# Weights split by the DMA that loads them: high parts rounded on the way in, low parts added onto the negated high parts

## The chip, the cores and the metric

The kernel runs on one core of a Trainium2 chip. The metric is the device time of one execution in microseconds (us), the median over the runs shown. A profile of one execution of the kernel before is at hand; times inside the kernel come from it.

## What is computed

One layer of a transformer block over 528 tokens (16 meta tokens and 512 real ones) of width 1024: an RMS norm, a projection into three attention branches (stick-breaking, indexed sparse with a top-k of 132 keys, differential) and three gates, the branches' output projections, an output matrix, a second norm and a gated feed-forward network with a convolution of width three. Cut to the two functions that hold the dense products:

```python
def _mixer(u, layer, w_in, ...):
    (q_sb, k_sb, v_sb, q_sp, k_sp, v_sp, q_ix, k_ix, w_ix,
     q_df, k_df, v_df, g_sb, g_sp, g_df) = _split_cols(u @ w_in)
    ...
    merged = (sigmoid(g_sb + b) * (y_sb @ w_br_sb) + sigmoid(g_sp + b) * (y_sp @ w_br_sp)
              + sigmoid(g_df + b) * (y_df @ w_br_df))
    return merged @ w_out

def _conv_ffn(u, w_up, conv_w, conv_b, w_down):
    z = u @ w_up
    gate, val = z[..., :D_FF], z[..., D_FF:]
    gp = jnp.pad(gate, ((0, 0), (CONV_WIDTH - 1, 0), (0, 0)))
    conv = conv_b + sum(gp[:, i:i + tp] * conv_w[i] for i in range(CONV_WIDTH))
    return (jax.nn.silu(conv) * val) @ w_down
```

All inputs are float32.

## The kernel before, in words

Activations lie transposed, features on the partitions, tokens along the free dimension. The weights are packed into 133 chunks of [128, 1024] float32, 512 KB each: eight tiles of 128 by 128. TensorE multiplies in the format float32r. To keep the precision of float32, every operand is split into a high part (the value rounded to float32r) and a low part (the value minus its high part), and every product is made in three passes: high by high, weight-high by activation-low, weight-low by activation-high (`mm3`, L309). A chunk of eight k-tiles is so 24 matmuls per half of the tokens; the low parts of its weights are read by the third pass alone.

The chunks are streamed in a fixed order (`order`, L277 to L287). `load` (L291) fetches a chunk with a DMA from SyncE's queue into a tile `wr` (three buffers). `prep` (L297) makes the two parts: ScalarE casts `wr` into `wh` (L304), and `sub` (L105) forms `wl = wr - wh` on VectorE or GpSimd, whichever a rough clock kept by the program takes to be free sooner; `wh` and `wl` have two buffers each. Every dense product first calls `prep` for its own chunk and for the next one, so that the split runs a chunk ahead, and `prep` starts the load two chunks ahead.

The first two chunks (`W_IX`, `W_QIX`) go along with the arrival of the input: the eight input tiles `hT` and halves of the two chunks alternate on SyncE's queue (L345 to L356), and a loop over the eight k-tiles (L382) emits, for each, the norm gain and split of the input tile (`xh` on ScalarE, `xl` on VectorE), at tiles 0, 1 and 4 the split of a part of the two chunks (`split`, L360: a cast on ScalarE, a subtraction on VectorE), the square of the tile for the norm, and 12 matmuls (`step`, L365).

TensorE runs in the order in which instructions are emitted: dense products with matmuls of attention streams between them, placed by the rough clock. The other engines run in order too; a tile framework sets the order on each of them from the emission order, its own estimate of when an instruction can start, and priorities, and puts in the semaphore waits. Two lines stand for many instructions in the profile, because helpers issue them: L97 for every operation of VectorE, ScalarE and GpSimd (`Timed.run`), L179 for every matmul (`mm`); L119 is `gdma`, a DMA issued by GpSimd. Groups are told apart by their tiles.

The feed-forward part (L1122 to L1142) runs 22 pairs of chunks. The gate chunk's product is evacuated by VectorE into `ft` tiles, convolved (one ScalarE operation, two on VectorE) and passed through SiLU on ScalarE; the value chunk's product is evacuated by VectorE, multiplied by the gate on GpSimd (`ft<-ft`, L1140), cast into `ah` on ScalarE and reduced to `al` by `sub`. The last 22 chunks multiply `ah` and `al` down to the output.

```python
    def prep(k):
        ...
        S.copy(wh, r)
        sub(wl, r, wh, HVW)
        wsp[k] = (wh, wl)
        load(after.get(after.get(k)))
```

Of the kernel before, what the change touches and what calls it, by code (L numbers as in the profile page):

```python
# [15 lines left out]
P = 128  # L16
D = 1024
T = 528            # meta tokens and real tokens
NM = 16
Q0 = 14            # first token whose mixer output is needed (the convolution reaches back two)  # L20
TQ = T - Q0        # 514 queries
HQ = TQ - 256      # 258: two meta queries and query blocks 0 and 1
# [11 lines left out]
# columns of the packed small parameters  # L34
# [4 lines left out]
# chunks of [128, 1024] in the packed weights  # L39
# [4 lines left out]
# the mixer's dense products in order: the projections of two heads' worth of a branch, four tiles  # L44
# of gates, half the columns of a branch's output
# [10 lines left out]
def tile_kernel(ctx: ExitStack, tc, hT, wpk, par, bias, yT):  # L56
# [3 lines left out]
    # ------------------------------------------------------------- order of emission  # L60
    # TensorE runs in the order in which its instructions are emitted here: dense products, with
    # the matmuls of other streams of work between them. A rough clock of the engines tells when a
    # stream's operands will be there, so that its matmuls come no earlier.
# [4 lines left out]
    SLACK = 1800    # from an operand's making by the clock to its matmul  # L68
    BSL = 500       # from a bank's last reading by the clock to its next use
    PACE = 12000    # for a round of the top-k  # L70
    TKS = 10000     # from the index part's making to its first product
    PRI = 100       # by how many instructions an evacuation goes ahead
    SET = 2200      # by how much earlier than SLACK the other engines' dependent steps come
    HVW = 1000      # VectorE's handicap against GpSimd for the weights' low parts
    HV = 500        # and for other differences
# [28 lines left out]

    def sub(out, a, b, hv=HV):  # L105
        """a - b in SBUF on VectorE, or on GpSimd where that is free sooner"""
        t = clock["P"]
        tv = max(clock["V"], t) + V.cost(out) + hv
        e = G if max(clock["G"], t) + G.cost(out) < tv else V
        e.tensor_tensor(out, a, b, OP.subtract)  # L110
# [16 lines left out]
    # ------------------------------------------------------------------ pools  # L127
# [13 lines left out]
    def bank(tag):  # L141
        """a PSUM bank, when one is free by the clock"""
        while sum(h["t"] + BSL > clock["P"] for h in held[tag]) >= banks[tag]:
            yield
        h = {"t": math.inf}
        held[tag].append(h)
        return ps.tile([P, 512], F32, tag=tag, bufs=banks[tag], name="ps" + tag), h
# [4 lines left out]
    # Slots that several streams of work share. A slot is taken here before the instructions  # L152
    # that fill it are emitted and given back after the last that reads it is, so an engine that
    # runs in the order of emission can't wait for one that is given back later.
# [30 lines left out]
    # ------------------------------- streams, which run between a dense product's matmuls  # L185
# [14 lines left out]
    def side_by_side(gens):  # L200
        """several streams in one; what each returns"""
# [16 lines left out]
    def settle(more=0):  # L218
        """until what the stream has emitted is done"""
# [4 lines left out]
    def ease(most=3000):  # L224
        """while VectorE is far behind"""
        while clock["V"] > clock["P"] + most:
            yield
# [11 lines left out]
    # -------------------------------------------------------------- constants  # L239
# [19 lines left out]
    # causal mask of a query block of 128 against columns c, the key at c standing at c - 400  # L259
    # from the block's first query  # L260
# [8 lines left out]
    # the two meta queries (14 and 15) against the meta keys  # L269
# [4 lines left out]
    # ------------------------------------------------------- weights, streamed  # L274
# [15 lines left out]

    def load(k):  # L291
        if k is not None and k not in wraw:
            r = wp.tile([P, 8, P], F32, tag="raw", bufs=3, name=f"wr{k}")
            nc.sync.dma_start(r, wpk[k].rearrange("p (j c) -> p j c", c=P))
            wraw[k] = r

    def prep(k):  # L297
# [3 lines left out]
        r = wraw[k]  # L301
        wh = wp.tile([P, 8, P], F32R, tag="wh", bufs=2, name=f"wh{k}")
        wl = wp.tile([P, 8, P], F32R, tag="wl", bufs=2, name=f"wl{k}")
        S.copy(wh, r)  # L304
        sub(wl, r, wh, HVW)
        wsp[k] = (wh, wl)
        load(after.get(after.get(k)))

    def mm3(out, prs, xh, xl, start=True, stop=True):  # L309
        """out += w^T x for the tiles j of chunk k and k-tiles kt of x, in three exact passes"""  # L310
# [13 lines left out]
    HALF = ((0, TH), (TH, TH))           # all tokens  # L324
    HALQ = ((0, HQ), (HQ, 256))          # queries, counted from token Q0

    # ------------------------------------------------ the input, and its norm's factors
# [3 lines left out]
    take("tmp", 10)  # L331
    for k in (W_IX, W_QIX):
        wraw[k] = wp.tile([P, 8, P], F32, tag="raw", bufs=3, name=f"wr{k}")
        wsp[k] = tuple(wp.tile([P, 8, P], F32R, tag=t, bufs=2, name=f"{t}{k}") for t in ("wh", "wl"))
# [6 lines left out]
    def load_half(k, a):  # L341
        nc.sync.dma_start(wraw[k][:, a:a + 4], wpk[k].rearrange("p (j c) -> p j c", c=P)[:, a:a + 4])

    # the order that gives TensorE work from the first tile of the input on
# [16 lines left out]
    def split(k, a, b):  # L361
        r, (wh, wl) = wraw[k], wsp[k]
# [3 lines left out]
    def step(k, ds, halves, q0, kt):  # L366
        """one k-tile of a tile of all its columns"""
# [12 lines left out]
    # the first two tiles go along with the input's arrival  # L380
# [17 lines left out]
    def rstd(dst, st, y0, a, now=True):  # L398
        """dst = (v + eps)^-0.5 from st = -v/2 in PSUM: Exp and Ln, then a Newton step"""
# [15 lines left out]
    # ------------------------------------------------ factors from the small parameters  # L415
# [6 lines left out]
    # -lambda of the differential attention on every partition  # L422
# [10 lines left out]
    # ------------------------------------- relative bias, by how far a key lies from the query  # L433
# [5 lines left out]
    def bias_stream():  # L439
# [3 lines left out]
        for e, r in enumerate(brd):  # L443
            # the table's high and low parts above each other, and the buckets of half the distances
# [14 lines left out]
        # a copy for each query, for the steps along which bias_tile reads  # L459
# [5 lines left out]
    def bias_tile(h):  # L465
        """[p, c]: the bias of query p against the key at column c (that is key c - 400 from the
        block's first query), or -1e30 where the key lies ahead"""
# [5 lines left out]
    # ----------------------------------------------------- dense tile of tokens  # L473
# [14 lines left out]
    # ---------------------------------------------------------------- index part  # L488
# [34 lines left out]
    for g in range(2):  # L523
# [15 lines left out]
        # the high, low and again the high parts of each head above each other, by way of DRAM  # L539
# [7 lines left out]
    # Each query's TOPK keys of the best score. Of the first block's 144 keys, the 144 - TOPK of the  # L547
# [684 lines left out]
```

## Time and profile before

| | |
|---|---|
| median of 3 runs | 931.87 us |
| lowest and highest run | 929.49 and 934.09 us |
| profiled execution: span from its first to its last instruction | 928.0 us |
| profiled execution: own time outside the span | not recorded; the median of the runs is 3.87 us above the span |
| TensorE matmuls busy | 901.2 us, 97% of the span, 6054 instructions |
| VectorE, ScalarE, GpSimd busy | 559.4, 456.7, 314.5 us (60%, 49%, 34%) |
| DMA engines | 91.44 MB, a mean of 99 GB/s |

A busy time of TensorE says that it was never without a matmul in flight, not that it ran at its peak. Idle time of an engine counts only where something that sets the end waits for it.

### The profile page before, as it was taken

What the parts mean: (1) busy time and instruction counts of PE and PEld (TensorE: products, weight loads), DVE (VectorE), ACT (ScalarE), POOL (GpSimd) and SP (SyncE); (2) the same over time, 40 slices, a digit from 0 to 9 for tenths busy, and PEclk for the clock granted to TensorE, in tenths of its full rate; (3) what the DMA queues carried; (4) which work ended last, traced back from release to release, by engine and by line L of the source; (5) the groups of instructions that cost most, each with busy time, mean ns of one, the idle gap of its engine ahead of it and who ended that gap; (6) DMA issues with size and microseconds to landing.
All of it is one profiled execution on the core that took longest, in us unless ns stands there. A gap on an engine that the chain in (4) does not pass through costs nothing.

```text
span 928.0 us, 15349 instructions
## 1 busy us (share of the span) xinstructions
PE 901.2 (97%) x6054; PEld 814.3 (88%) x6054; DVE 559.4 (60%) x1129; ACT 456.7 (49%) x848; POOL 314.5 (34%) x185
## 2 busy tenths in 40 slices
PE   7989989899999999999998999999999999999998
PEld 6987988799998889988998999999999999888886
DVE  6599999985578655797437445555555555422221
ACT  7476686668377787644545444333333333311110
POOL 2433232343433424666235323344444333200100
PEclk9999999999999999999999999999999999999999
DMA  6584112142333212331222532223223233333330
GB/s 227 149 237 156 47 69 69 48 125 66 101 104 92 82 63 80 99 97 48 68 78 87 178 91 91 92 91 91 91 91 91 92 96 95 106 113 102 114 102 23
DMA packets 30439, 91.44 MB, mean 99 GB/s; under 512 B 3929, under 2 KB 4073, under 8 KB 30368
## 3 DMA queue, kind: packets, MB, share of 16 engines
q1 hardware_dynamic: 29648, 88.05, 31.0%
q0 software_dynamic: 720, 2.42, 0.9%
q8 instruction: 47, 0.77, 0.3%
q14 instruction: 24, 0.20, 0.1%
HBM read 80.88 MB, written 5.86 MB: 93 GB/s over the span
## 4 chain that ended last, share of the span: by engine, by line
PE 77%; DVE 14%; DMA 4%; ACT 2%; issue 1%; SPq 1%; POOL 0%; DVEq 0%; POOLq 0%; ACTq 0%
PE psd L179 52%; PE psw L179 23%; DVE tmp L97 7%; DVE work L97 2%; DVE m L97 2%; PE psw L183 2%; ACT tmp L97 1%; DMA qd<-tmp 1%; DVE G L97 1%; DMA qk<-qk 1%; DVE pm L97 1%; DMA wr<-wpk 1%; DVE pt L97 1%; DMA qst<-qd 1%; DMA gd<-tab 1%
## 5 line engine op out<-in xcount | busy, mean ns | idle before, releaser
L97 POOL TENSOR_TENSOR wl<-wr,wh 128x1024 fp32r<-128x1024 f32 x75 | 181.3, 2418 | 347.7 <-ACT wh L97 226.7
L97 ACT CAST wh<-wr 128x1024 fp32r<-128x1024 f32 (+2 forms) x137 | 139.2, 1018 | 178.4 <-PE psd L179 123.6
L179 PE MATMUL psd<-xh,wh 128*128 128x258 f32 (+2 forms) x792 | 119.5, 291 | 3.7 <-DVE tmp L97 2.5
L179 PE MATMUL psd<-xh,wl 128*128 128x258 f32 (+2 forms) x792 | 118.6, 290 | 0.0
L179 PE MATMUL psd<-xl,wh 128*128 128x258 f32 (+2 forms) x792 | 118.5, 290 | 0.0
L97 DVE TENSOR_TENSOR wl<-wr,wh 128x1024 fp32r<-128x1024 f32 (+3 forms) x62 | 72.3, 1168 | 69.4 <-PE psd L179 60.2
L179 PEld LDWEIGHTS psd<-xh,wh 128*128 128x128 f32 x792 | 103.8, 189 | 7.5 <-DVE tmp L97 1.8
L179 PEld LDWEIGHTS psd<-xh,wl 128*128 128x128 f32 x792 | 103.1, 189 | 3.3
L179 PEld LDWEIGHTS psd<-xl,wh 128*128 128x128 f32 x792 | 103.5, 190 | 2.9 <-issue 0.2
L97 ACT ACTIVATE tmp<-tmp 128x528 f32<-128x528 f32 (+7 forms) x154 | 69.7, 475 | 23.1 <-DVE tmp L97 20.5
L97 POOL TENSOR_TENSOR ft<-ft 128x512 f32<-128x512 f32 x22 | 46.5, 2115 | 82.5 <-DVE ft L97 79.1
L97 DVE SCALAR_TENSOR_TENSOR ft<-ft,prm 128x512 f32<-128x512 f32 x44 | 58.2, 1324 | 20.3 <-ACT ft L97 19.6
L179 PE MATMUL psw<-qk 128*128 128x400 f32 (+4 forms) x192 | 55.8, 339 | 2.3 <-DVE tmp L97 1.6
L179 PEld LDWEIGHTS psw<-qk 128*128 128x128 f32 (+1 forms) x192 | 32.2, 168 | 19.9 <-issue 6.2
L179 PE MATMUL psw<-uh,wh 128*128 128x256 f32 (+2 forms) x264 | 47.0, 320 | 0.0
L179 PE MATMUL psd<-ul,wh 128*128 128x258 f32 (+2 forms) x264 | 46.9, 319 | 0.0
L179 PE MATMUL psw<-ul,wh 128*128 128x256 f32 (+2 forms) x264 | 46.9, 319 | 0.0
L179 PE MATMUL psd<-uh,wl 128*128 128x258 f32 (+2 forms) x264 | 46.9, 319 | 0.0
L179 PE MATMUL psw<-uh,wl 128*128 128x256 f32 (+2 forms) x264 | 46.8, 319 | 0.0
L179 PE MATMUL psd<-uh,wh 128*128 128x258 f32 (+2 forms) x264 | 46.8, 319 | 0.0
L179 PE MATMUL psd<-ah,wl 128*128 128x512 f32 x176 | 45.6, 395 | 0.0
L179 PE MATMUL psd<-ah,wh 128*128 128x512 f32 x176 | 45.6, 395 | 0.0
(195 smaller groups left out, 1645.8 us busy)
## 6 DMA issues: line engine op xcount, KB each, us to landing
wr<-wpk SPq DMA_DIRECT2D x131, 512.0 KB, 3.5
qk<-qk SPq DMA_DIRECT2D x24, 132.0 KB, 3.0
gd<-tab SPq DMA_DIRECT2D x8, 328.0 KB, 5.2
tmp<-hT SPq DMA_DIRECT2D x8, 264.0 KB, 6.8
W<-gd POOLq DMA_DIRECT2D x8, 264.0 KB, 4.2
qk<-tmp SPq DMA_DIRECT2D x16, 128.5 KB, 2.6
hm<-hT SPq DMA_DIRECT2D x8, 257.0 KB, 3.8
yT<-ft SPq DMA_DIRECT2D x8, 256.0 KB, 2.1
```

The costliest lines, as they stand in the source:

```text
L97: return f(out, *a, **k)
L179: PE.matmul(out, lhsT, rhs, **k)
L183: PE.transpose(out, x, ident[:x.shape[0], :x.shape[0]])
```

## The change

The chunks are no longer loaded as they are and split by engines. `load` now fetches a chunk with a DMA issued by GpSimd whose destination is float32r, so that the transfer rounds: what lands is `wh`. The low part is made by `low`: ScalarE writes the negated high part into `wl`, and a second DMA issued by GpSimd loads the same chunk again and adds it onto `wl`, which leaves w - wh. The casts `wh<-wr` and the subtractions `wl<-wr,wh` of these 131 chunks are gone, and the tiles `wr` with them: `wh` has four buffers and `wl` three (before: `wr` three, `wh` two, `wl` two). `prep(k)` now makes the low part of `k` and of the next chunk and loads the one after it; since every dense product calls it for its own and for the next chunk, low parts are made two chunks ahead and high parts loaded three ahead. The first two chunks keep their loads, casts and subtractions; their unsplit tiles lie in slots of `wh` and `wl`. The program's clock books 1050 ns of GpSimd for each of the two DMAs.

```diff
+    def chunk(k):
+        return wpk[k].rearrange("p (j c) -> p j c", c=P)
+
     def load(k):
         if k is not None and k not in wraw:
-            r = wp.tile([P, 8, P], F32, tag="raw", bufs=3, name=f"wr{k}")
-            nc.sync.dma_start(r, wpk[k].rearrange("p (j c) -> p j c", c=P))
-            wraw[k] = r
-
-    def prep(k):
+            wh = wp.tile([P, 8, P], F32R, tag="wh", bufs=4, name=f"wh{k}")
+            gdma(wh, chunk(k))
+            wraw[k] = wh
+
+    def low(k):
         if k is None or k in wsp:
             return
         load(k)
-        r = wraw[k]
-        wh = wp.tile([P, 8, P], F32R, tag="wh", bufs=2, name=f"wh{k}")
-        wl = wp.tile([P, 8, P], F32R, tag="wl", bufs=2, name=f"wl{k}")
-        S.copy(wh, r)
-        sub(wl, r, wh, HVW)
-        wsp[k] = (wh, wl)
-        load(after.get(after.get(k)))
+        wl = wp.tile([P, 8, P], F32R, tag="wl", bufs=3, name=f"wl{k}")
+        S.activation(wl, wraw[k], AF.Copy, scale=-1.0)
+        book("G", 1050)
+        nc.gpsimd.dma_start(wl, chunk(k), accum_op=OP.add)
+        wsp[k] = (wraw[k], wl)
+
+    def prep(k):
+        if k is None:
+            return
+        low(k)
+        a = after.get(k)
+        load(after.get(a))
+        low(a)
...
+    raws = {}
     for k in (W_IX, W_QIX):
-        wraw[k] = wp.tile([P, 8, P], F32, tag="raw", bufs=3, name=f"wr{k}")
-        wsp[k] = tuple(wp.tile([P, 8, P], F32R, tag=t, bufs=2, name=f"{t}{k}") for t in ("wh", "wl"))
+        raws[k] = wp.tile([P, 8, P], F32, tag="wl" if k else "wh", bufs=3 if k else 4, name=f"wr{k}")
+        wsp[k] = tuple(wp.tile([P, 8, P], F32R, tag=t, bufs=4 if t == "wh" else 3, name=f"{t}{k}") for t in ("wh", "wl"))
+        wraw[k] = wsp[k][0]
```

How this moves instructions is shown at three places.

ScalarE at the start of the program, before: `xh` is the scaled input tile, `wh_110` and `wh_113` the high parts of the first two chunks, `tmp<-tmp` the squares for the norm.

```order
L97 ACTIVATE xh<-tmp,prm 128x528
L97 CAST wh_110<-wr_109 128x128
L97 CAST wh_110<-wr_109 128x384
L97 ACTIVATE tmp<-tmp 128x528
L97 CAST wh_113<-wr_112 128x128
L97 CAST wh_113<-wr_112 128x384
L97 ACTIVATE xh<-tmp,prm 128x528 x2
```

The same place with the change:

```order
L97 ACTIVATE xh<-tmp,prm 128x528
L97 ACTIVATE tmp<-tmp 128x528
L97 ACTIVATE xh<-tmp,prm 128x528 x2
L97 ACTIVATE tmp<-tmp 128x528 x2
L97 ACTIVATE xh<-tmp,prm 128x528
L97 CAST wh_110<-wr_109 128x128
L97 CAST wh_113<-wr_112 128x128
```

The first cast of a weight, which stood behind one input tile, now stands behind four. No line of the diff says so; the framework ordered it anew.

GpSimd in the feed-forward part, before (`ft<-ft` is the product of gate and value; VectorE makes the low parts that are missing here):

```order
L97 TENSOR_TENSOR wl_7148<-wr_7001,wh_7147 128x1024
L97 TENSOR_TENSOR ft<-ft 128x512
L97 TENSOR_TENSOR wl_7248<-wr_7151,wh_7247 128x1024
L97 TENSOR_TENSOR ft<-ft 128x512
L97 TENSOR_TENSOR wl_7348<-wr_7251,wh_7347 128x1024
```

The same place with the change (L119 are the rounding loads, L309 the adding ones; `wl_8492` belongs to `wh_8455`, a value chunk, and `wl_8555` to `wh_8490`, a gate chunk):

```order
L119 DMA wh_8455<-wpk 128x1024
L309 DMA wl_8457<-wpk 128x1024
L119 DMA wh_8490<-wpk 128x1024
L97 TENSOR_TENSOR ft<-ft 128x512
L309 DMA wl_8492<-wpk 128x1024
L119 DMA wh_8553<-wpk 128x1024
L309 DMA wl_8555<-wpk 128x1024
L119 DMA wh_8588<-wpk 128x1024
```

Four DMAs stand where one subtraction stood, and the adding DMA of each value chunk comes behind the product `ft<-ft`.

ScalarE in the feed-forward part, before (`ft<-ft,prm` and the next row are the convolution's first tap and SiLU):

```order
L97 ACTIVATE ft<-ft,prm 128x512
L97 ACTIVATE ft<-ft 128x512
L97 CAST wh_7883<-wr_7787 128x1024
L97 CAST ah<-ft 128x512
L97 CAST wh_7947<-wr_7851 128x1024
```

The same place with the change:

```order
L97 ACTIVATE ft<-ft,prm 128x512
L97 ACTIVATE ft<-ft 128x512
L97 ACTIVATE wl_8492<-wh_8455 128x1024
L97 CAST ah<-ft 128x512
L97 ACTIVATE wl_8555<-wh_8490 128x1024
```

The negation takes the place of the cast, at the same points between SiLU and `ah`.

## Rows read from the trace of the kernel before

**Rows 1.** The page, busy time of each engine, its share of the span, instructions.

```profile
PE 901.2 (97%) x6054; PEld 814.3 (88%) x6054; DVE 559.4 (60%) x1129; ACT 456.7 (49%) x848; POOL 314.5 (34%) x185
```

**Rows 2.** Busy time by stage (us): PE, PEld, DVE, ACT, POOL; clock, DMA share, GB/s.

```profile
100.00:200.00 100.00, 94.07 (x698) 86.43 (x698) 99.34 (x233) 67.82 (x130) 34.38 (x18) 0.98 0.22 65
...
400.00:511.00 111.00, 108.32 (x814) 100.30 (x814) 68.72 (x157) 53.69 (x92) 53.48 (x33) 0.98 0.24 75
...
568.00:800.00 232.00, 232.00 (x1471) 209.38 (x1470) 122.33 (x144) 83.52 (x104) 93.04 (x41) 1.00 0.30 92
```

**Rows 3.** Groups of GpSimd, ScalarE and VectorE by form: count, busy us, mean ns, idle before.

```profile
L97 POOL TENSOR_TENSOR wl<-wr,wh 128x1024 fp32r<-128x1024 f32 x75 | 181.3, 2418 | 347.7 <-ACT wh L97 226.7 <-PE psd L179 82.6 <-ACT tmp L97 17.5
L119 POOL DMA_DIRECT2D W<-gd x8 | 4.4, 556 | 26.5 <-DVE mx L97 14.6 <-DMA gd<-tab 9.3 <-DVE work L97 2.3
L97 ACT CAST wh<-wr 128x1024 fp32r<-128x1024 f32 x131 | 136.6, 1043 | 176.9 <-PE psd L179 123.6 <-issue 31.2 <-PE psw L179 18.7
L97 DVE TENSOR_TENSOR wl<-wr,wh 128x1024 fp32r<-128x1024 f32 x56 | 69.4, 1239 | 67.4 <-PE psd L179 60.2 <-ACT wh L97 7.2
```

**Rows 4.** Timeline of the start: start us, us, engine, line, operation, count, idle before.

```profile
4.03 0.43 SPq L339 DMA_DIRECT2D tmp<-hT  x1
4.72 0.69 ACT L97 CAST wh<-wr 128x128 fp32r<-128x128 f32 x2
5.06 0.81 PE L179 MATMUL psw<-xh,wh 128*128 128x264 f32 x2 [5.06 <-ACT wh L97]
9.04 1.46 ACT L97 ACTIVATE xh<-tmp,prm 128x528 fp32r<-128x528 f32 x2 [0.55 <-DMA tmp<-hT]
10.92 1.17 ACT L97 ACTIVATE tmp<-tmp 128x528 f32<-128x528 f32 x2
11.99 0.72 ACT L97 ACTIVATE xh<-tmp,prm 128x528 fp32r<-128x528 f32 x1
21.23 1.05 PE L179 MATMUL psw<-tmp,onesd 128*128 128x264 f32 x4
```

**Rows 5.** Busy time within the start, columns as in Rows 2.

```profile
5.05:8.14 3.09, 1.87 (x7) 1.45 (x7) 1.26 (x4) 1.37 (x4) 0.27 (x2) 1.00 0.91 229
8.14:11.90 3.76, 3.72 (x14) 3.12 (x14) 2.92 (x6) 3.21 (x6) 0.00 (x0) 1.00 1.04 373
11.90:21.12 9.22, 9.22 (x78) 9.22 (x77) 9.09 (x21) 8.19 (x17) 0.00 (x0) 1.00 0.66 255
```

**Rows 6.** Timeline of one pair of the feed-forward chunks, columns as in Rows 4.

```profile
653.72 1.13 PE L179 MATMUL psw<-uh,wh 128*128 128x258 f32 x8
653.92 0.69 DVE L97 TENSOR_TENSOR ft<-psd,rs 128x512 f32<-128x512 f32 x1 [1.57 <-PE psd L179]
654.75 2.14 POOL L97 TENSOR_TENSOR ft<-ft 128x512 f32<-128x512 f32 x1 [3.75 <-DVE ft L97]
659.43 2.03 PE L179 MATMUL psw<-uh,wh 128*128 128x512 f32 x8
663.16 2.04 PE L179 MATMUL psw<-uh,wl 128*128 128x512 f32 x8
665.03 1.13 PE L179 MATMUL psd<-uh,wh 128*128 128x258 f32 x8
```

**Rows 7.** DMA in 568 to 800: queue, packets, MB, engines' share; issues, KB, us to landing.

```profile
q1 hardware_dynamic: 5825, 21.19, 29.5%
wr<-wpk SPq DMA_DIRECT2D x41, 512.0 KB, 3.5
```

**Rows 8.** A DMA issue in 30 to 100, columns as in Rows 7.

```profile
qd<-tmp SPq DMA_DIRECT2D x4, 257.0 KB, 7.4
```

**Rows 9.** Low parts by engine: ns min/median/max, first and last start; stretches 100:200, 400:511.

```profile
L97 POOL TENSOR_TENSOR wl<-wr,wh x12: 2379/2394/2683, 99.4 to 197.5; 128x1024 fp32r<-128x1024 f32 x12
L97 DVE TENSOR_TENSOR wl<-wr,wh x6: 1206/1220/1791, 402.0 to 495.2; 128x1024 fp32r<-128x1024 f32 x6
```

**Rows 10.** Waits of TensorE in 400 to 511: us in total, times, longest us.

```profile
PE psd L179 <- DVE ml L97: 2.6, 2, 1.9
```

More of the change, by code (lines that the diff above doesn't have):

```diff
@@ L341, in load_half @@
     def load_half(k, a):
-        nc.sync.dma_start(wraw[k][:, a:a + 4], wpk[k].rearrange("p (j c) -> p j c", c=P)[:, a:a + 4])
+        nc.sync.dma_start(raws[k][:, a:a + 4], chunk(k)[:, a:a + 4])
     nc.sync.dma_start(prm[:, :C_QSP], par[:, :C_QSP])
@@ L361, in split @@
     def split(k, a, b):
-        r, (wh, wl) = wraw[k], wsp[k]
+        r, (wh, wl) = raws[k], wsp[k]
         S.copy(wh[:, a:b], r[:, a:b])
```

## The prediction

> **What bounds the kernel now.** Read the page first: TensorE is busy for 901.2 of 928.0 us [rows 1], so at most 26.8 us of the span can be won without touching the products themselves. Then the table by stage [rows 2], where busy time is to be held against the length of each stretch. From 568 to 800, the feed-forward part, TensorE is busy for all 232.0 us, with VectorE at 122, GpSimd at 93 and the DMA engines at 0.30: nothing that other engines are spared there can shorten it. In 100 to 200, where the top-k runs, TensorE idles for 5.9 us and VectorE is busy for 99.3 of 100. In 400 to 511 TensorE idles for 2.7 us. So the change, which spares VectorE and GpSimd work, can only win where TensorE waits for them, and it loses wherever weights come later than they did. Those two places must be found.
>
> **What is removed.** 75 subtractions on GpSimd, 181.3 us, and 56 on VectorE, 69.4 us [rows 3]. On ScalarE nothing goes: 131 casts at 1.04 us become 131 negations of the same shape. What of it lay on the path? In 100 to 200, where VectorE is the late engine, the 12 low parts made there were all GpSimd's [rows 9], so VectorE is spared nothing; that idle time stays. In 400 to 511 VectorE loses 6 subtractions at 1.22 us [rows 9], 7.3 us, and the wait of TensorE on VectorE there is 2.6 us, for the low parts of the merged activations [rows 10]. I credit **-1.0 us** (ends: 0 and -2.6). From 511 on nothing is credited, since TensorE is never idle before its last chunks.
>
> **What is added on GpSimd.** 262 DMA issues. The row of a DMA that GpSimd issues, with 128 rows, is 556 ns [rows 3]: 146 us in all, less than the 181.3 us removed. Their number is not what costs, but their place, below.
>
> **The start.** Before, the first cast of a weight ran at 4.72 and the first matmul at 5.06 [rows 4]. Now that cast stands behind four input tiles on ScalarE. The timeline gives their times: the second and third tile came in for 9.04, their scaling took 1.46 and their squares 1.17, which ends at 11.7; the fourth tile's load was issued at 4.03, its scaling takes 0.72, a cast 0.35. TensorE begins at 12.8. The products of the first two chunks are 96 matmuls; in 11.90 to 21.12 it ran 78 in 9.22 us, 0.118 each [rows 5], so 11.3 us if all go at that pace. The early ones did not: 7 in 1.87 and 14 in 3.72 us, 0.27 each, though the granted clock in these rows is 1.00, that is 2.4 GHz. For 14 such matmuls I add 2.1 us (ends: none, and 21 of them, 3.1). The rounding load of the third chunk is now issued by GpSimd before the small bias table, in the first microseconds, when the DMA engines were 0.91 busy at 229 GB/s [rows 5]. Its 524 kB cost the inputs up to 2.3 us; I take 0.9. The first stage then ends at 12.8 + 0.9 + 11.3 + 2.1 = 27.1 instead of 21.1, after which the norm's matmuls came [rows 4, 5]: **+6.0 us** (ends: 12.8 + 11.3 gives +3.0; with 2.3 and 3.1 it is +8.4). Nothing later takes it back, since VectorE's busy stretch starts from the same products.
>
> **The feed-forward pairs.** Here the order on GpSimd decides: the adding DMA of a value chunk stands behind the product `ft<-ft`. The timeline of one pair [rows 6]: a value chunk ends at 653.72, its evacuation at 654.61, the product runs from 654.75 to 656.89; the adding DMA is issued until 657.45 (0.56). TensorE wants that low part in the third pass of the next value chunk, at 663.16. So **5.7 us** remain for the DMA to land. The pair takes 665.03 - 653.72 = 11.31 us, and whatever the landing exceeds 5.7 us by is added to each pair, since the next product waits for the end of the delayed chunk. A gate chunk's adding DMA is issued shortly after and wanted only within the chunk that begins at 665.03, so it binds later.
>
> How long does an adding DMA take to land? No row shows one. A plain load of 512 KB lands 3.5 us after its issue [rows 7]: the lower end. It must also read the tile that it adds to. 41 loads took 29.5% of the engines over 232 us [rows 7], 1.67 us of all engines each; if the second read only takes that much, 3.5 + 1.67 = 5.2. If it is like a second load after the first, 7.0. If the result's writing is a third one, 10.5, the upper end (257 KB to memory took 7.4 us in a crowded stretch [rows 8]). I take the middle of 5.2 and 7.0, 6.1 us, since reading a tile in the core is nearer to a load than to a crowded write. Then 0.4 us is missing in each of 22 pairs: **+8.8 us** (ends: 0 and 22 x 4.8 = 106).
>
> The Trainium skill, page "Collectives: The Full Stack", section "The bandwidth ceiling: the fold count and why AG ≠ RS ≠ AR", says that an add in the DMA engines is slow not by its arithmetic but because it reads two sources, which doubles the read traffic. By that rule the adding DMA takes 3.34 us of the engines and lands at 5.2, and the sum would be +5.0 instead of +13.8; no run here shows it yet.
>
> **The sum.** -1.0 + 6.0 + 8.8 = +13.8 us. The profiled span of 928.0 becomes 941.8. The median of the runs is 3.87 us above that span, and I carry that over: 931.87 + 13.8 = **945.7 us**, 1.5% slower. From one measurement of this kernel to the next about 0.5%, 4.7 us, can't be told from no change.
>
> **Rivals.**
> *The landing fits.* If the adding DMA lands within 5.7 us, the pairs stay at 11.31 and only the start counts: +5.0, 936.9 us, and 933 where the start comes out at its low end. For it: GpSimd issues both DMAs into one queue, the adding one ahead of the next load, so they need not share. Against it: the margin is half a microsecond over the best case.
> *The DMA engines become the bound.* Each chunk now needs two transfers. At 1.67 us for a rounding load and 3.34 for two reads that is 5.0 of the 5.66 us that a chunk takes: it fits. If rounding too halves the rate, 3.34 + 3.34 = 6.7, and 1.0 us is missing in each of the 8 + 44 + 22 = 74 chunks from the output matrix on: 931.9 + 5 + 77 = 1014 us. For it: two unknown rates, little room. Against it: 373 GB/s were reached in 8.14 to 11.90 [rows 5], so 1.67 us is not a floor.
> *GpSimd becomes the bound.* If an issue costs as much as a subtraction, 2.4 us [rows 3], four issues and the product make 11.7 us of a pair's 11.31, +9 us over 22 pairs: 946 us with the start. A reason would be that VectorE holds GpSimd up. The Trainium skill, page "SBUF — State Buffer", section "Who interferes with whom", says that VectorE in its two-port modes shuts GpSimd out for a whole instruction. In 100 to 200, with VectorE 99% busy, GpSimd's subtractions had a median of 2394 ns and a longest of 2683 [rows 9], so the trace shows 0.3 us of that at most.
> *Faster.* SyncE's queue loses 131 loads, and VectorE work: if the idle time of 100 to 200 and of 400 to 511 went (8.6 us) and the start cost its low 3.0, the time would be 926.3. Against it: VectorE loses nothing in 100 to 200. That the change does less than it says is excluded by the new order, which has 131 DMAs of each kind.
>
> **How the numbers follow.** Forecast 0.40, the landing fits 0.25, DMA-bound 0.25, GpSimd-bound 0.05, faster 0.05. The second lies about the 0.5% line: half of it counts as slower (0.13), half as no change (0.12). Slower: 0.40 + 0.25 + 0.05 + 0.13 = 0.83; same 0.12; faster 0.05. The range goes from 931, below the fitting case, to 1014, the middle of the DMA-bound one; left out are the faster case and the upper half of the DMA-bound one, under 0.2. The forecast's own range is 937 (nothing missing in the pairs) to 966 (a landing at 7.0).
>
> **What would show it.** In the profile after: the first matmul at 12 to 14 us instead of 5, and the norm's matmuls at 25 to 29; adding DMAs with a median landing near 6; in the feed-forward part a wait of TensorE for a DMA in the third pass of value chunks, 0 to 1 us each, and a DMA share near 0.8. The forecast is wrong if TensorE's waits come in every chunk and the DMA share is at 1, or if the pairs still take 11.31 us.

## The result, and the profile after

Four runs of the changed kernel took 937.82 to 943.11 us, median **940.42**; the kernel before, beside them, 931.65. The ratio is 1.0101, 95% interval 1.0070 to 1.0131: 1.0% slower, inside the predicted range and 5 us under the predicted 945.7. The profiled execution has a span of 939.0 us, 11.0 more than before. The page's first line, against [rows 1]:

```profile
PE 904.9 (96%) x6054; PEld 819.2 (87%) x6054; DVE 430.9 (46%) x1075; ACT 458.5 (49%) x848; POOL 292.2 (31%) x370
```

TensorE is busy 3.7 us longer with the same 6054 matmuls and idle 7.3 us longer. VectorE lost 128.5 us of busy time, though only 69.4 us of subtractions were taken from it. The table by stage, columns as in [rows 2], of before for three stretches not shown yet:

```profile
30.00:52.00 22.00, 21.86 (x180) 21.44 (x179) 12.50 (x19) 8.42 (x18) 9.57 (x4) 1.00 0.71 172
52.00:100.00 48.00, 42.77 (x308) 38.42 (x308) 46.73 (x108) 33.37 (x94) 13.08 (x9) 1.00 0.57 172
200.00:300.00 100.00, 99.24 (x734) 91.11 (x732) 66.13 (x179) 66.30 (x148) 36.19 (x20) 1.00 0.32 93
```

and of after:

```profile
30.00:52.00 22.00, 20.82 (x172) 20.36 (x170) 8.34 (x23) 9.05 (x17) 5.10 (x7) 1.00 1.03 240
52.00:100.00 48.00, 40.75 (x267) 37.24 (x267) 31.65 (x89) 25.75 (x80) 12.23 (x14) 0.89 0.96 238
100.00:200.00 100.00, 100.00 (x764) 92.65 (x764) 98.43 (x256) 78.68 (x152) 22.44 (x30) 1.00 0.63 132
200.00:300.00 100.00, 96.08 (x678) 87.98 (x678) 49.70 (x157) 58.47 (x127) 24.22 (x32) 0.95 0.70 149
400.00:511.00 111.00, 111.00 (x828) 102.04 (x827) 64.05 (x164) 59.25 (x110) 51.10 (x57) 0.98 0.66 136
568.00:800.00 232.00, 232.00 (x1473) 209.54 (x1473) 76.62 (x128) 85.96 (x107) 83.90 (x103) 1.00 0.85 185
```

Length less busy time is TensorE's idle time; the stretches are equal in time, and the same work lies up to 11 us later in the changed kernel. From before to after it changes by +6.2 us in 0 to 30, +3.1 in 30 to 100, -5.9 in 100 to 200, +4.4 in 200 to 400, -0.6 in 400 to 568, and by nothing between 568 and 800. With the 3.7 us of slower matmuls (granted clock 0.89 in 52 to 100 and 0.95 in 200 to 300, against 1.00 in both) that is the 11 us. The first matmul of the feed-forward part comes 10.5 us later (561.4, before 550.9) and the last one of the kernel 10.8 us later, so nearly all of it arises ahead of the feed-forward part. TensorE's waits in the whole execution (engine, line, what it waited for; us in total, times, longest):

```profile
PE psw L179 <- ACT wh L97: 13.4, 1, 13.4
PE psw L179 <- DMA qst<-qd: 7.2, 1, 7.2
PE psw L179 <- DMA qk<-qk: 6.2, 3, 2.4
PE psd L179 <- DVE ml L97: 1.9, 2, 1.3
```

The first is the start, as predicted (timeline, columns as in [rows 4]; the norm's matmuls came at 21.23 before):

```profile
13.39 0.81 PE L179 MATMUL psw<-xh,wh 128*128 128x264 f32 x2 [13.39 <-ACT wh L97]
...
27.17 1.05 PE L179 MATMUL psw<-tmp,onesd 128*128 128x264 f32 x4
```

The second and third were not predicted: activations that go by a DMA to memory and back (the index part's queries, stored to `qd` and reloaded to `qst`), or from one half of the partitions to the other (`qk`, the attention's q and k). The chain of waits, 28 to 60 (start, us, what):

```profile
28.57 7.54 DMA wh<-wpk
36.22 1.06 ACT wl L97
37.28 0.30 ACT tmp L97
37.61 0.45 DVE tmp L97 x2
38.06 10.54 DMA qd<-tmp
48.66 0.31 SPq L558
49.02 8.88 DMA qst<-qd
58.04 1.10 PE psw L179 x4
```

A negation waits for its rounding load, a cast of the index part's queries stands behind it on ScalarE, and then the queries take 10.5 us to memory and 8.9 back, among DMA engines with a share of 1.03 in 30 to 52 and 0.96 in 52 to 100 (0.71 and 0.57 before, where the chain has 7.5 and 4.9 us). Two causes are mixed in it: ScalarE's order and the crowd of DMAs. The wait costs more than its own length: behind it, in 58 to 62, the granted clock is 0.50, that is 1.2 GHz, and eight matmuls of 264 columns take 2.06 us, against 1.13 ahead of it.

The feed-forward pairs, [rows 6], did not change: chunks start at 653.22 and 664.53, 11.31 us apart. GpSimd and TensorE in such a pair:

```profile
654.29 1.28 POOL L97 TENSOR_TENSOR ft<-ft 128x512 f32<-128x512 f32 x1 [1.93 <-DVE ft L97]
655.53 0.88 POOL L309 DMA_DIRECT2D wl<-wpk  x1
...
653.22 1.13 PE L179 MATMUL psd<-uh,wh 128*128 128x258 f32 x8
658.93 2.03 PE L179 MATMUL psd<-uh,wh 128*128 128x512 f32 x8
662.66 2.03 PE L179 MATMUL psd<-uh,wl 128*128 128x512 f32 x8
664.53 1.12 PE L179 MATMUL psw<-uh,wh 128*128 128x258 f32 x8
666.46 1.12 PE L179 MATMUL psw<-uh,wl 128*128 128x258 f32 x8
```

and the DMAs of 568 to 800 (queue, packets, MB, engines' share; issues, KB, us to landing):

```profile
q0 software_dynamic: 11753, 42.77, 84.8%
...
wh<-wpk POOLq DMA_DIRECT2D x42, 512.0 KB, 4.6
wl<-wpk POOLq DMA_DIRECT2D x41, 512.0 KB, 5.7
```

### The profile page after: what moved, and what is told of

Read it like the earlier page. It is cut to its first block, busy times and chain, and to the rows that moved or that the text cites. A ratio compares the mean times of both kernels' runs of the same rounds, so it can differ in the third digit from the quotient of the medians.

```text
span 939.0 us, 15404 instructions
## 1 busy us (share of the span) xinstructions
PE 904.9 (96%) x6054; PEld 819.2 (87%) x6054; DVE 430.9 (46%) x1075; ACT 458.5 (49%) x848; POOL 292.2 (31%) x370
## 4 chain that ended last, share of the span: by engine, by line
PE 82%; DMA 8%; DVE 5%; ACT 2%; issue 1%; POOL 1%; SPq 0%; ACTq 0%; POOLq 0%; DVEq 0%
PE psd L179 55%; PE psw L179 25%; DMA qk<-qk 3%; PE psw L183 2%; DVE tmp L97 2%; DVE work L97 2%; DMA wh<-wpk 2%; DMA qd<-tmp 1%; DMA qst<-qd 1%; DMA tmp<-hT 1%; DVE m L97 1%; ACT wl L97 1%; ACT tmp L97 1%; DVE G L97 0%; POOL tmp L97 0%
## 5 line engine op out<-in xcount | busy, mean ns | idle before, releaser
L97 ACT ACTIVATE wl<-wh 128x1024 fp32r<-128x1024 f32 x131 | 138.7, 1059 | 268.1 <-PE psd L179 176.8
L309 POOL DMA_DIRECT2D wl<-wpk x131 | 114.4, 873 | 201.1 <-ACT wl L97 177.0
L119 POOL DMA_DIRECT2D wh<-wpk x131 | 73.4, 561 | 318.8 <-PE psd L179 220.6
L179 PE MATMUL psd<-xh,wl 128*128 128x258 f32 (+2 forms) x792 | 121.1, 295 | 0.0
L179 PEld LDWEIGHTS psd<-xh,wl 128*128 128x128 f32 x792 | 106.0, 194 | 3.0 <-issue 0.2
L97 ACT ACTIVATE tmp<-tmp 128x528 f32<-128x528 f32 (+7 forms) x154 | 69.7, 475 | 15.9 <-DVE tmp L97 11.2
L97 DVE TENSOR_TENSOR ft<-hm,psd 128x512 f32<-128x512 f32 x8 | 5.5, 689 | 114.8 <-PE psd L179 114.8
L97 DVE SCALAR_TENSOR_TENSOR ft<-ft,prm 128x512 f32<-128x512 f32 x44 | 33.1, 752 | 30.8 <-ACT ft L97 30.0
L179 PE MATMUL psd<-al,wh 128*128 128x512 f32 x176 | 45.6, 395 | 0.0
## 6 DMA issues: line engine op xcount, KB each, us to landing
qk<-tmp SPq DMA_DIRECT2D x16, 128.5 KB, 3.6
```

Source lines behind the costliest of these rows:

```text
L97: return f(out, *a, **k)
L119: nc.gpsimd.dma_start(out, x)
L179: PE.matmul(out, lhsT, rhs, **k)
L309: nc.gpsimd.dma_start(wl, chunk(k), accum_op=OP.add)
```

## The experiments

Each is a small edit of the changed kernel.

### e1: the start put back

```diff
     load_h(6, 7)
-    load(order[2])
...
+    load(order[2])
     load(order[3])
```

> The changed kernel with one line moved: the rounding load of the third chunk is emitted after the loop over the input tiles instead of before it, which puts the first casts of weights back behind one input tile on ScalarE. Theory (the start costs what the order on ScalarE costs): first matmul at 5 instead of 13.39 us, the norm's matmuls at 21 to 22.5 instead of 27.17, and the time 5 to 6 us under the changed kernel, 934 to 936 us. Rival A (it is the early rounding load, which takes DMA time from the input): that load is still issued among the first, so the norm's matmuls stay at 25 or later and the time at 938 or more. Rival B (given back later: TensorE then waits longer for the index part's queries): the norm's matmuls at 21, but the wait for qst grows from 7.2 us towards 13, and the time stays at 939 to 941 us.

Measured: 934.71 us, ratio to before 1.0039 (1.0020 to 1.0058). The first matmul comes at 5.01 and the norm's at 22.19:

```profile
5.01 0.81 PE L179 MATMUL psw<-xh,wh 128*128 128x264 f32 x2 [5.01 <-ACT wh L97]
...
22.19 1.05 PE L179 MATMUL psw<-tmp,onesd 128*128 128x264 f32 x4
```

The order on ScalarE at the start cost 5.7 us, and neither rival holds: the third chunk's load is issued at 2.82 us in both kernels, and the wait for qst is 5.4 us, not more. Why the framework puts the casts back when this load is emitted later is open. With the start mended, the kernel is still 0.4% slower than before.

### e2: two negations behind the index part's casts

```diff
-        S.activation(wl, wraw[k], AF.Copy, scale=-1.0)
+        i = S.activation(wl, wraw[k], AF.Copy, scale=-1.0)
+        if k in order[4:6]:
+            tc.keep_in_program_order(i)
...
         load(after.get(a))
-        low(a)
+        if a not in held_low:
+            low(a)
```

Here `held_low` is the fifth chunk until the index part's casts are emitted, and nothing after.

> The changed kernel with two negations, those of the fifth and sixth chunk, moved on ScalarE behind the casts of the index part. Theory (ScalarE's order: the negation that waits 7.5 us for its rounding load holds up the casts whose results go to DRAM and back): the first store to qd is issued some 8 us earlier, at 29 to 31 instead of 38.06, TensorE's wait for qst falls from 7.2 to under 1 us, and the time by 6 to 9 us, to 932 to 935 us. Rival (the DMA engines are full from 30 to 52, share 1.03, so it doesn't matter when the stores are issued): stores and reloads still take 11 and 9 us or more, the wait stays at 4 us or more, and the time at 937 us or more.

Measured: 938.81 us, ratio 1.0075 (1.0051 to 1.0099), which can't be told from the changed kernel's 1.0101. Its profiled execution was the fastest of its five (934.49), so its small wait for qst (1.6 us) need not hold for the others; its chain:

```profile
36.45 4.62 DMA qd<-tmp
...
43.72 16.65 DMA qst<-qd
60.51 0.32 PE psw L179
```

The stores start 1.6 us earlier (36.45, not 38.06), not 8, because the other casts and VectorE's steps end only then. The stores now take 4.62 us instead of 10.54, but the reloads 16.65 instead of 8.88. By the medians ScalarE's order was a small part, and the crowd remains; that the other four executions were slow by the same wait is not shown.

### e3 and e4: the adding DMA of the feed-forward part delayed

```diff
         G.tensor_tensor(a[:, :512], a[:, :512], c[:, :512], OP.mult)
+        for _ in range(2):
+            more.append(G.tensor_tensor(c[:, :512], a[:, :512], a[:, :512], OP.mult).ins)
```

with five in e4, and the adding DMA of the gate chunk after the next one tied behind them.

> The changed kernel with two more products of the same shape on GpSimd behind each product of gate and value, ahead of the adding DMA that follows it; they write to a tile that nothing reads again, and the output is unchanged. Each takes 1.3 us alone, up to 2.1 beside VectorE, so this DMA is issued 2.6 to 4.2 us later in each of 20 pairs. As the prediction read it (the DMA brings the next value chunk's low part, wanted at 662.66 in the pair that I read after; it lands at 655.53 + 5.7 = 661.2, 1.4 us to spare): 1.2 to 2.8 us per pair, 24 to 56 us in all, 964 to 996 us. As re-read (TensorE's own rows use this low part with 258 and 256 columns, so it is the gate chunk's after the next value chunk, wanted at 666.46, 5.2 us to spare): pairs stay at 11.31 us, and the time at 938 to 943 us.

> As the run with two more products, but with five: this adding DMA is issued 6.5 to 10 us later in each pair. As the prediction read it (1.4 us to spare): 5 us or more per pair, over 100 us in all. As re-read (5.2 us to spare, and the delay of a gate chunk comes back to GpSimd only two pairs on): it is missed by 1.3 us or more, which makes 0.6 us or more per pair, a time of 953 us or more, with TensorE waiting in the third pass of gate chunks (258 columns) alone; at products of 2.1 us it would be some 2.5 us per pair and GpSimd near 100% busy in this stretch, 995 us.

Measured, one run each: 945.49 and 945.43 us. In e3 TensorE is busy for 232.0 of 232 us in 568 to 800, and pairs take 11.31 us. Its time is above the 938 to 943 expected, but its feed-forward part already starts 5.1 us later than the changed kernel's (566.5, not 561.4), and nothing ahead of that part was edited (TensorE is busy 37.4 of 48 us in 52 to 100). In e4 TensorE is idle for 3.9 us in 568 to 800, in short waits:

```profile
PE psd L179 <- DMA wl<-wpk: 1.9, 3, 1.0
PE psw L179 <- DMA wl<-wpk: 1.6, 2, 1.2
```

All five stand in the third pass of gate chunks (258 columns). The extra products took 1.2 us each. In the pair that I read, e4 issues this DMA at 660.17, 8.2 us after the value chunk's end at 651.98, against 2.3 us in the changed kernel (655.53, 653.22). It is 5.9 us later, just over the 5.2 us to spare. From its first high-by-high matmul to its last the feed-forward part takes 253.8 us, against 246.2 in the changed kernel, so the delay costs 7.6 us, nothing like the 100 us of the first reading. The re-reading holds. (I had set 953 us or more for e4: the misses came out shorter, and its feed-forward part happened to start 2.9 us earlier than the changed kernel's.)

### e5: the adding DMA left out

```diff
-        nc.gpsimd.dma_start(wl, chunk(k), accum_op=OP.add)
```

> The changed kernel without its adding DMAs: the low parts of 131 chunks stay the negated high parts, so the third pass of their products multiplies other numbers than the reference's; everything else is as in the changed kernel. It prices the two DMAs apart. In 568 to 800 the changed kernel keeps the engines 0.85 busy with both, 4.74 us of all engines per chunk of 5.66 us. If an adding DMA costs two reads and a rounding load one (1.67 us, as a plain load before): the share falls to 0.30. If a rounding load costs as much as an adding one: to 0.42. For the index part: if the crowd of adding DMAs makes the stores and reloads slow, the reloads (qst) take 6 us or less instead of 8.9, TensorE's wait for them falls from 7.2 to 3 us or less, and that for qk from 6.2 to 1 or less. If not the crowd but ScalarE's order alone makes them late, the wait stays at 5 us or more.

Measured, one run: 917.6 us, 23 under the changed kernel; in its profile 14.3 us less idle time of TensorE, and 8.9 us less of busy time. No wait of TensorE for any DMA is left; the clock is 1.00 in every stretch. In 568 to 800:

```profile
q0 software_dynamic: 5926, 21.59, 32.7%
...
wh<-wpk POOLq DMA_DIRECT2D x41, 512.0 KB, 3.8
```

So a rounding load takes 32.7% of 232 us over 41, **1.85 us** of all engines (1.67 for a plain one, [rows 7]), and the adding DMA the rest of 84.8%, about **2.9 us**, 1.6 times a rounding load, if a rounding load costs the same beside it. The reloads (qst) still took 9.1 us between 30 and 100, against my 6, but the stores 4.1, and that was enough. The stores are issued no earlier than in e2 (36.18 and 35.98), so what e5 wins over e2 here is not ScalarE's order. The waits for qk are gone too, with nothing changed in the program's clock. The crowd that the adding DMAs make is the larger loss of this change, 23 us against 5.7 for the start; e5, which makes no low parts, is 13 us under the kernel before.

### e6 to e8: some chunks split as before, with other buffers

The chunks in a set `old` keep the plain load, the cast and the subtraction; to make room, all high parts were put into three buffers and the low parts into four (two rings of two, by turns).

```diff
-        if k is not None and k not in wraw:
-            wh = wp.tile([P, 8, P], F32R, tag="wh", bufs=4, name=f"wh{k}")
+        if k in old and k not in wraw:
+            wraw[k] = wp.tile([P, 8, P], F32, tag="raw", bufs=3, name=f"wr{k}")
+            nc.sync.dma_start(wraw[k], chunk(k))
+        elif k is not None and k not in wraw:
+            wh = wp.tile([P, 8, P], F32R, tag="raw", bufs=3, name=f"wh{k}")
...
-        wl = wp.tile([P, 8, P], F32R, tag="wl", bufs=3, name=f"wl{k}")
...
+        t = ("wh", "wl")[len(wsp) % 2]
+        wl = wp.tile([P, 8, P], F32R, tag=t, bufs=2, name=f"wl{k}")
```

> The first six of the 131 chunks, whose products run until about 60 us, are split as before the change (plain load from SyncE's queue, cast, subtraction); the other 125 as in the changed kernel, with three buffers for high and four for low parts. Theory (the change loses its time at the start and in the index part, by order and by a crowd of DMAs, and wins in 100 to 200 and 400 to 511, where VectorE is no longer slowed by GpSimd): the start is back (norm's matmuls at 21 to 22), the wait for qst is gone, the granted clock in 52 to 100 is back at 1.00, TensorE's idle time in 100 to 200 stays at 1 us or less; 4 to 6 us remain as waits for qk. 931.65 - 5.9 - 2.7 + 4.4 = 927.5, between 925 and 930 us, faster than both kernels. Rival (the crowd only moves: the seventh and later chunks' adding DMAs meet the table copies and the qk moves in 50 to 100): TensorE idles 4 us more there, and the time is 931 to 935 us.

> As the run with the first six, but with the first twelve chunks split as before. Theory: the crowd in 30 to 100 is gone altogether, and with it the loss; what is given up is that GpSimd's subtractions slow VectorE down in 60 to 110, while the top-k runs: TensorE's idle time of 5.9 us in 100 to 200 comes back by 1 to 3 us. 926 to 930 us. If it is 2 us or more under the run with the first six, the crowd still cost that one something; if it is 2 us or more above, VectorE's freedom in the top-k's first part is worth more than the crowd costs.

> All chunks ahead of the feed-forward part are split as before, the 66 of the feed-forward part as in the changed kernel. As re-read (an adding DMA has 5 us to spare in a pair, and TensorE is never idle there): no effect, 930 to 933 us. As the prediction had it (0.4 us missing in each of 22 pairs): 940 us, and with the pairs at 11.7 us.

Measured: 1042.93, 1047.23 and 1004.22 us, ratios 1.1205, 1.1241 and 1.0797. All three expectations failed alike: TensorE waits for low parts, 59, 58 and 44 us. So they leave open what they were made for, and led to the next.

### e9: three buffers for high parts

```diff
-            wh = wp.tile([P, 8, P], F32R, tag="wh", bufs=4, name=f"wh{k}")
+            wh = wp.tile([P, 8, P], F32R, tag="wh", bufs=3, name=f"wh{k}")
...
-        wl = wp.tile([P, 8, P], F32R, tag="wl", bufs=3, name=f"wl{k}")
+        wl = wp.tile([P, 8, P], F32R, tag="wl", bufs=4, name=f"wl{k}")
```

> The changed kernel with three buffers for high parts and four for low parts, instead of four and three; nothing else. The runs with the first six and twelve chunks and with the feed-forward part alone had this split of buffers too. Theory (a rounding load waits for a high part's buffer to come free, then come its landing of 4.6 us, the negation and the adding DMA of 5.7 us: with three buffers this chain starts a chunk of 5.7 us later and no longer fits): TensorE waits 2 to 5 us for low parts in many third passes, 60 to 110 us in all, 1000 to 1050 us. Rival (what hurt those runs was chunks of two kinds side by side): within 5 us of the changed kernel, 936 to 945 us.

Measured, one run: 1067.26 us.

```profile
PE psw L179 <- DMA wl<-wpk: 38.9, 15, 5.0
PE psd L179 <- DMA wl<-wpk: 28.1, 17, 3.0
```

It is slower than the 1000 to 1050 us expected, and the rival is out. So the pairs keep 11.31 us by the fourth buffer of the high parts. With three, load, negation and adding DMA run in a row from the end of a chunk, and the low part is late, as the prediction feared for another reason: in one pair the load is issued at 700.21 us, the negation starts at 706.86, the adding DMA at 708.22, and the third pass, 3.9 us late, at 713.87. Its matmuls are slower too: 941.9 us busy at a mean clock of 0.952.

### e10 to e12: a version that loses neither

The first twelve chunks are split as before, their unsplit tiles in the slots of the high parts (four and three buffers stay); the start is that of e1; and the program's clock gives the moves of q and k 9000 ns to land instead of 5000.

```diff
+    old = set(order[2:14])
...
+        if k in old and k not in wraw:
+            wraw[k] = wp.tile([P, 8, P], F32, tag="wh", bufs=4, name=f"wr{k}")
+            nc.sync.dma_start(wraw[k], chunk(k))
...
-        unit["t"] = max(unit.get("t", 0), cur[0]["t"] + 5000)
+        unit["t"] = max(unit.get("t", 0), cur[0]["t"] + 9000)
```

> The first twelve chunks are split as before the change, with their unsplit tiles in the slots of the high parts, so that four high and three low parts stay for the other 119 chunks, which are split as in the changed kernel; the third chunk's load stands behind the loop over the input, and the program's clock allows 9000 instead of 5000 ns for the moves of q and k to land. Theory (the loss is made by order at the start, by the crowd of DMAs in 30 to 100 and by the moves of q and k; the gain is VectorE's freedom): the start at 21 to 22 us, no wait for qst over 1 us, granted clock 0.98 or more in 52 to 100, idle time in 100 to 200 between 0 and 2 us, waits for qk of 2 us or less, and the feed-forward part without idle time: 914 to 924 us, faster than both kernels. Rival (adding DMAs cost TensorE time in each stretch where they run, 200 to 800 too): 928 us or more.

> As the run with the first twelve chunks in their own rings, but with the first twenty split as before, which carries GpSimd's subtractions on to about 170 us, through most of the top-k. Theory (VectorE is slowed by GpSimd's subtractions while the top-k runs): TensorE's idle time in 100 to 200 comes back towards 5.9 us, and this run is 2 to 5 us slower than the one with twelve. Rival (the gain in 100 to 200 comes from something else): within 1 us of the run with twelve, or faster.

> As the run with the first twelve chunks in their own rings, but with the first six split as before: six more chunks, from about 60 to 100 us, go by two DMAs, while tables and moves of q and k still crowd the engines there and the top-k begins. If VectorE's freedom counts for more: TensorE's idle time of 2.5 us in 100 to 200 goes, and the time is 919 to 923 us. If the crowd counts for more: TensorE waits for DMAs in 52 to 100 (for qk or low parts, 2 us or more), the clock falls under 0.96 there, and the time is 927 us or more. Within 923 and 927 us neither outweighs the other.

Measured: e10 **924.78 us**, ratio to before 0.9922 (0.9906 to 0.9939), faster than both kernels; e11 with twenty chunks 931.77, 1.0007 (0.9991 to 1.0022); e12 with six 925.88, 0.9934 (0.9911 to 0.9958). In e10 the waits for qst and qk are gone, though the time is 0.8 us above what I expected, with the norm's matmuls at 22.75, and 2.4 us of idle time and a clock of 0.96 in 52 to 100. In 100 to 200, first e10, then e11:

```profile
100.00:200.00 100.00, 97.54 (x736) 90.74 (x735) 94.40 (x245) 72.08 (x136) 28.35 (x33) 0.98 0.61 134
```

```profile
100.00:200.00 100.00, 94.32 (x675) 86.91 (x675) 98.49 (x238) 70.03 (x134) 32.43 (x22) 0.93 0.27 73
```

Eight chunks more by the old way bring the idle time of 100 to 200 back, from 2.5 to 5.7 us, though the DMA share there falls from 0.61 to 0.27; the clock falls from 0.98 to 0.93, and the kernel loses 7 us by the medians (2 to 5 were expected; the two profiled executions are 3.1 us apart). In e12 that idle time is 0.5 us, but 52 to 100 has 5.9 us of it at a clock of 0.89. TensorE waits there for ScalarE, not for a DMA itself; the chain behind ScalarE holds moves of q and k of 11.2 and 7.3 us. Crowd and freedom about balance each other. What the longer allowance for q and k is worth by itself was not run.

## Why the prediction came out where it did

The time was right, its working only in part: by its own last sentence (the pairs still take 11.31 us) the forecast was wrong. That the time still lies near it is luck: a term of +8.8 that wasn't there and a gain of 5.9 that was missed were offset by losses that were not in the sum (3.1, 4.4 and 3.7 us, below).

- **The start**, +6.0: right. The first matmul came at 13.39 (12.8 forecast), the norm's at 27.17 (27.1), and e1 takes 5.7 us back.
- **The pairs**, +8.8: wrong, 0. The adding DMA lands in 5.7 us, close to the 6.1 assumed, and its share of 0.85 is near the 0.8 forecast. What failed is the step "TensorE wants that low part in the third pass of the next value chunk". I took the low part behind the product, `wl_8492`, for a value chunk's, and the part ahead of this prediction says so as well. TensorE's instructions, in their order in the program, show that it belongs to a gate chunk, since it is used with 258 columns, not 512:

```
1075 L179 MATMUL psw<-uh,wl_8457 128x512 x8
1076 L179 MATMUL psd<-uh,wh_8455 128x258 x8
1077 L179 MATMUL psd<-ul,wh_8455 128x258 x8
1078 L179 MATMUL psd<-uh,wl_8492 128x258 x8
```

  The product that stands ahead of it belongs to the pair two before its use. Issued at 655.53, wanted at 666.46, it has 10.9 us and 5.2 to spare, not -0.4. e3 and e4 bear that out; in these pairs the rival "the landing fits" was the true one, though by slack that it did not count on (its low time should read 933.9, not 933). e9 shows on what it rests: the fourth buffer.
- **"That idle time stays"** in 100 to 200: wrong, all 5.9 us went. VectorE lost no subtraction there, as I said, but several of its operations with two inputs in SBUF got faster, since GpSimd subtracts no more (below).
- **-1.0** for 400 to 511: about right, -0.6 by 568.
- **The index part and the moves of q and k**: not in the sum at all. I priced the DMA engines for the feed-forward part, where TensorE never waits, and not for 30 to 100, whose share of 0.71 in 30 to 52 before would have told: with 2.9 us more for each chunk there was no room. That cost 3.1 us more idle time in 30 to 100, 4.4 in 200 to 400, and the 3.7 us of matmuls at a lower clock.
- **The engines as the bound**: not reached; 4.74 us of 5.66 per chunk. The Trainium skill, page "Collectives: The Full Stack", section "The bandwidth ceiling: the fold count and why AG ≠ RS ≠ AR", says of collectives that an add reads two sources and so doubles the read traffic; twice a rounding load, an estimate by that rule, would be 3.7 us. The trace gives about 2.9, less than that estimate.
- **GpSimd**: 131 issues of 561 ns and 131 of 873, not 262 of 556: 188 us instead of 146. No wait of TensorE in the profile is for GpSimd.

## What to carry to other kernels

When work moves from engines to DMAs, price the DMA engines stage by stage, and first where other transfers lie on the path; the stage in which the new DMAs are most numerous was the one that didn't care. To find when a tile is wanted, read the consumer's own rows, not the neighbours of its producer. And when a chain of load, change and add stands ahead of its use, count its buffers: one fewer for the high parts, though one more for the low parts, made this kernel 127 us slower, in one run.

## What was not expected of the hardware

GpSimd and VectorE slow each other far more than the 0.3 us that the prediction allowed. I had taken that from GpSimd's subtractions ([rows 9]), which are the side that isn't held up. VectorE in the feed-forward part, of before, the convolution's taps, then two of them and GpSimd's subtraction beside them in the timeline:

```profile
L97 DVE SCALAR_TENSOR_TENSOR ft<-ft,prm 128x512 f32<-128x512 f32 x42 | 56.2, 1337 | 19.4 <-ACT ft L97 18.6
...
649.63 2.72 DVE L97 SCALAR_TENSOR_TENSOR ft<-ft,prm 128x512 f32<-128x512 f32 x2 [0.89 <-ACT ft L97]
...
648.60 2.40 POOL L97 TENSOR_TENSOR wl<-wr,wh 128x1024 fp32r<-128x1024 f32 x1 [3.02 <-ACT wh L97]
```

of after, the same and two others (busy us, mean ns):

```profile
L97 DVE SCALAR_TENSOR_TENSOR ft<-ft,prm 128x512 f32<-128x512 f32 x42 | 31.6, 752 | 29.4 <-ACT ft L97 28.6
L97 DVE TENSOR_TENSOR al<-ft,ah 128x512 fp32r<-128x512 f32 x20 | 13.9, 693 | 43.2 <-ACT ah L97 43.2
L97 DVE TENSOR_TENSOR ft<-psd,rs 128x512 f32<-128x512 f32 x10 | 6.9, 692 | 21.5 <-PE psd L179 21.5
```

and of e4, whose extra products keep GpSimd busy for 135 us in this stretch:

```profile
L97 DVE TENSOR_TENSOR al<-ft,ah 128x512 fp32r<-128x512 f32 x20 | 22.4, 1118 | 95.0 <-ACT ah L97 95.0
L97 DVE TENSOR_TENSOR ft<-psd,rs 128x512 f32<-128x512 f32 x10 | 6.9, 690 | 5.1 <-PE psd L179 5.1
```

With GpSimd's subtraction beside them the taps took 1337 ns, without it 752. The two taps at 649.63 end at 652.35, which is 1.35 us after the subtraction's end at 651.00: two taps take 1.54 without it, so the first had hardly got on before that end. GpSimd was held up in turn: its product at 654.75, begun inside VectorE's subtraction of 654.53 to 655.75, took 2.14 us [rows 6], after the change 1.28. In e4 the subtraction with both inputs in SBUF goes from 693 to 1118 ns, and the evacuation, whose one input is in PSUM, stays at 690. The Trainium skill, page "SBUF — State Buffer", section "Who interferes with whom", says that a VectorE instruction with two SBUF inputs contends with a GpSimd instruction that reads SBUF, and that the order of issue decides which of the two is held up. The trace agrees: 1337 against 752 ns for the taps that begin behind a subtraction, and 692 for the evacuation before and after alike. The prediction had cited the rule beside it, on two-port modes, and missed this one. In 100 to 200, where it decides, the mean of VectorE's four `tmp<-tmp` operations of 128x528 falls with the number of GpSimd's subtractions in that stretch: 2271 ns at 12 (before), 1736 at 9 (e11), 1096 at 2 (e10), 702 at none (after). Before and after:

```profile
L97 DVE TENSOR_TENSOR tmp<-tmp 128x528 f32<-128x528 f32 x4 | 9.1, 2271 | 0.0
...
L97 DVE TENSOR_TENSOR tmp<-tmp 128x528 f32<-128x528 f32 x4 | 2.8, 702 | 0.0
```

Not every such operation is held up: those of 128x400 keep their time (559 and 562 ns).
